# Moving the angle tables, pacing the linear work through two attentions, and adding the band term in VectorE's pass

## The chip, the cores and the metric

The kernel runs on one core of a Trainium2 chip. The metric is the device time of one execution in microseconds. Engines are named as in the profile: PE is TensorE (PEld its weight loads), DVE is VectorE, ACT is ScalarE, POOL is GpSimd, SP is SyncE, which only issues DMAs here.

## What is computed

The reference is two blocks over 512 positions of width 1024, all in fp32. The first block mixes a pooling branch and a causal block attention (8 heads) and has an MLP of width 4096 with a squared ReLU. The second has two layers: differential attention (8 heads of two softmaxes over all 512 keys), then windowed attention with 16 query heads, 4 key heads and a sink logit for each head; each layer is followed by a gated convolution MLP (2 x 2816) and a gated projection of a side input. The windowed attention, cut to what matters:

```
mask = (abs(kpos - qpos) <= 128) & (kpos >= 0) & (kpos < S)
s = where(mask, q k^T * d**-0.5, -inf)
m = maximum(max(s), sink)
e = exp(s - m)
pr = e / (sum(e) + exp(sink - m))
o = pr v
```

## The kernel before

Every large product is made of three fp32r matmuls: each operand is split into a high and a low half (`w_split`, `split`: the high half by ScalarE or GpSimd, the low by VectorE's subtraction), and `mm3` (lines 102 to 107) adds high x high, low x high and high x low in a PSUM bank. Activations lie transposed, 1024 features in eight tiles of 128 x 512 positions. `linear_steps` (line 123) walks over the output columns, 128 at a time: for each it loads and splits weights some tiles ahead (four high and four low buffers), makes 8 x 3 matmuls of 512 columns, and evacuates. It is a generator and yields after each `mm3`.

PSUM has tags: `mm` (2 banks), `sc` (2, scores), `pv` (1, values), `st` (1, statistics), `tr` (2, transposes). `wide` says which of them a linear product may use: 5 is all of `mm`, `sc`, `pv`; 1 is `mm` alone; 4 is `mm` and `sc`.

In both attentions of the second block, `weave` (line 163) writes linear work (`lin()`) between attention steps (`att()`). A list of points (step, us) says how much linear work, in an estimate of its own (648 ns for one `mm3`), has been written when a step is reached. Marks hold either side back: `("sq", g, i)` says that a head's queries are written, `"scored"` and `"scored2"` that the last scores are, `("o", k)` and `("so", k)` that a tile of the attention's output is. This sets the order of the program text. The framework that builds the program plans each engine's order from it: what is written first goes first, and an engine that would stand idle in the plan takes later work that is ready.

The angle tables for the rotations (`late_consts`, line 261) are made by VectorE and two sines on ScalarE and stored to DRAM. They are written behind the first of four up-projections of the first MLP (line 762). The rows of the convolution weights are loaded next (line 764) and transposed behind the second up-projection (line 766); the tables' buffers lie where these rows' buffers come to lie after them. Behind the first four columns of the first up-projection `mid` writes the statistics of the norm, and the fifth bank takes the fifth column meanwhile.

In the windowed attention one step of 64 handles 128 queries of one head against 256 or 384 keys. `scores` (line 1131) makes two matmuls of scores, and a third one that adds the band (0 inside, -1e30 outside) as identity x band, over those blocks that the band cuts. VectorE then negates the scores and takes the minimum together with the negated sink (line 1150), ScalarE makes the exponential from the bank and its sum (line 1152). After every second step the sink's exponential, the sum and the reciprocal are made for two steps together (lines 1156 to 1158), and GpSimd scales the two probability tiles. Those are a ring of six (`pr`). `flip` transposes them five steps after their scores, `values` multiplies with V once for a head. Queries and keys are rotated in `rope` (line 800), with DMAs that swap halves, and restacked by further DMAs. The residual stream is spilled to DRAM during each attention and reloaded by `unspill`.

Of the kernel before, what the change touches and what calls it, by code (L numbers as in the profile page):

```python
# [17 lines left out]
KT = D // 128  # L18
# [15 lines left out]
class Net:  # L34
# [647 lines left out]
    def block1(self):  # L682
# [58 lines left out]
        with tc.tile_pool(name="mlp", bufs=1) as M:  # L741
# [4 lines left out]
            for g in range(FF1 // 1024):  # L746
# [14 lines left out]
                if g == 0:  # L761
                    self.late_consts()
                    cv = ExitStack()
                    rows = self.conv_rows(cv.enter_context(tc.tile_pool(name="cv", bufs=1)))
                if g == 1:
                    self.conv_cols(rows)
                    cv.close()
                if g == 3:
                    self.sq_start()
# [108 lines left out]
    def diff(self):  # L878
# [4 lines left out]
        with tc.tile_pool(name="diff", bufs=1) as P:  # L883
# [17 lines left out]
            def lin():  # L901
                for h in range(KT):
                    if h != 1:
                        yield from qk(h)
                    if h in (0, 1, 4, 6):
                        i = (0, 1, 4, 6).index(h)
                        if i >= 2:
                            yield ("dvfree", i - 2)
                        yield from vv(i)
                yield "scored"  # L910
                self.unspill()
                self.wide = 4
                yield from self.linear_steps(a["diff_w_o_2"][0], o, [n * 128 for n in range(KT)], evac_o, group=3,
                                             ready=lambda k: ("o", k))
# [96 lines left out]
            def att():  # L1011
                for g in range(39):
                    yield g
                    if g < 32:
# [6 lines left out]
                        if g == 31:  # L1021
                            self.marks.add("scored")
# [24 lines left out]
            self.weave(att(), lin(), [(0, 50), (24, 125), (28, 126), (34, 134), (38, 139)])  # L1047
            self.wide = 5

    def swa(self):  # L1050
# [5 lines left out]
        with tc.tile_pool(name="swa", bufs=1) as P:  # L1056
            sink = P.tile([128, 4 * HQ], F32, name="sink")[:, :HQ]
            nc.scalar.dma_start(sink, a["swa_sinks_2"].to_broadcast([128, HQ]))
            identr = P.tile([128, 128], F32R, name="identr")
            nc.vector.tensor_copy(identr, self.ident)  # L1060
            nsink = P.tile([128, 4 * HQ], F32, name="nsink")[:, :HQ]
            nc.vector.tensor_scalar(nsink, sink, -1.0, None, op0=OP.mult)
            band = P.tile([128, 384], F32R, name="band")
            z = P.tile([128, 384], F32, name="pr", tag="pr", bufs=6)
            nc.gpsimd.memset(z, 0.0)
            nc.gpsimd.affine_select(z, z, pattern=[[1, 384]], compare_op=OP.is_ge, fill=NEG, base=0,
                                    channel_multiplier=-1)
            nc.gpsimd.affine_select(band, z, pattern=[[-1, 384]], compare_op=OP.is_ge, fill=NEG, base=256,
# [47 lines left out]
            def lin():  # L1116
                yield from self.linear_steps(w, self.u, [1024, 1152], evac_k, group=2)
                yield from q_steps(0, 0)
                yield from self.v_steps(w, 1280, rs()[0], lambda t: (V[:, t, :, 0], V[:, t, :, 1]), self.u)
                for g, j in ((0, 1), (1, 0), (1, 1)):  # L1120
                    yield from q_steps(g, j)
                yield "scored2"
                self.unspill()
                self.wide = 4
                yield from self.linear_steps(a["swa_w_o_2"][0], o, [n * 128 for n in range(KT)], evac_o, group=3,
# [5 lines left out]
            def scores(n, t):  # L1131
# [11 lines left out]
                for step in range(2):  # L1143
                    self.dots(sc, Q[g, i], K[g], s, qs, ks, step)
                blk = lambda x: x.rearrange("p (b q) -> p b q", q=128)
                m0, m1 = (1 if t == 0 else 0), (1 if t == NT - 1 else b1 - b0)
                c = b0 - t + 1
                nc.tensor.matmul(blk(sc)[:, m0:m1:2], identr, blk(band)[:, c + m0:c + m1:2], start=False, stop=True)
                p = P.tile([128, 384], F32, name="pr", tag="pr", bufs=6)
                nc.vector.tensor_scalar(p[:, :w_], sc, -1.0, nsink[:, h:h + 1], op0=OP.mult, op1=OP.min,  # L1150
                                        accum_out=st[:, 1, t:t + 1])
                nc.scalar.activation(p[:, :w_], sc, AF.Exp, bias=st[:, 1, t:t + 1], accum_out=st[:, 2, t:t + 1])  # L1152
                PR[n, t] = p
                if t % 2:
                    ts = slice(t - 1, t + 1)
# [3 lines left out]
                    for t_ in (t - 1, t):  # L1159
# [39 lines left out]
            def att():  # L1199
                done = []  # L1200
                for g in range(70):
                    yield g
                    if g < 64:
# [6 lines left out]
                        if g == 63:  # L1210
                            self.marks.add("scored2")
# [4 lines left out]
                    if g >= 9 and (g - 9) % 4 == 0:  # L1216
                        n = (g - 9) // 4
                        values(n)
# [16 lines left out]
            self.weave(att(), lin(), [(0, 35), (50, 63), (63, 63), (69, 85)])  # L1235
# [285 lines left out]
```

## Time and profile before

| what | value |
| --- | --- |
| time, median of 3 runs | 2008.62 us (2007.45 to 2009.44) |
| profiled execution | 2005.98 us |
| its span, first to last instruction | 2004.2 us |
| TensorE busy | 1955.9 us |
| VectorE busy | 1262.3 us |
| ScalarE busy | 799.9 us |
| GpSimd busy | 443.8 us |
| mean granted TensorE clock | 0.997 |

Busy time is the union of an engine's instructions. Matmuls are pipelined and their ends are modelled, so the distance from one start to the next says more than a duration. In a row, what stands behind `<-` at the end is what the engine had waited for.

### The profile page before, as it was taken

Reading aid. Unit: us, or ns where it says so; the run is one execution under the profiler, and the core shown is the slowest. Engines: PE = TensorE matmul, PEld = TensorE weight load, DVE = VectorE, ACT = ScalarE, POOL = GpSimd, SP = SyncE. Lnnn points to the kernel's source line nnn. Section 1 sums busy time; section 2 is a strip of 40 time slices with the busy share of each in tenths; the row PEclk is TensorE's granted clock in tenths of the full one; section 3 lists DMA queues with packets and bytes.
Section 4 is the critical chain, followed back from the end, with each engine's and each line's share of the span. In section 5 each row is a group of like instructions: output and inputs, shape, how many; then the busy total and the mean of one; then the engine's idle time right before and its main releaser. Section 6 shows DMA issues by size and latency. Waiting matters only on the chain.

```text
span 2004.2 us, 25430 instructions
## 1 busy us (share of the span) xinstructions
PE 1955.9 (98%) x9386; PEld 1621.8 (81%) x9386; DVE 1262.3 (63%) x2087; ACT 799.9 (40%) x1392; POOL 443.8 (22%) x545
## 2 busy tenths in 40 slices
PE   8999999899999999999999999999998999999997
PEld 6897778787888887887788888887877788888886
DVE  6447655534434468988684565668798684565665
ACT  4335434322212445554342331334575342342342
POOL 4125421000000211110221113122343221113122
PEclk9999999999999999999999999999999999999999
DMA  5263543332323356543332323335522333334231
GB/s 195 85 171 77 157 135 120 107 105 80 110 86 104 116 173 154 129 128 93 102 106 87 106 87 102 90 121 168 141 78 89 85 105 105 94 96 143 78 105 63
DMA packets 263853, 224.33 MB, mean 112 GB/s; under 512 B 9957, under 2 KB 236338, under 8 KB 263730
## 3 DMA queue, kind: packets, MB, share of 16 engines
q1 hardware_dynamic: 260538, 218.19, 36.7%
q10 hardware_dynamic: 3192, 4.52, 0.7%
q8 instruction: 74, 1.21, 0.3%
q14 instruction: 49, 0.40, 0.1%
HBM read 182.83 MB, written 14.16 MB: 98 GB/s over the span
## 4 chain that ended last, share of the span: by engine, by line
PE 51%; DVE 6%; ACT 2%; issue 1%; DMA 1%; SPq 0%; POOL 0%; DVEq 0%; ACTq 0%; POOLq 0%
PE mm L105 7%; PE mm L107 7%; PE mm L106 7%; PE sc L107 6%; PE sc L105 6%; PE sc L106 6%; PE pv L105 3%; PE pv L106 3%; PE pv L107 3%; PE sc L849 1%; DVE wlo L94 1%; PE pv L858 1%; ACT pr L1152 1%; DVE Tl L80 1%; DVE st L955 0%
## 5 line engine op out<-in xcount | busy, mean ns | idle before, releaser
L94 DVE TENSOR_TENSOR wlo<-wst,whi 128x1024 fp32r<-128x1024 f32 (+2 forms) x304 | 392.1, 1293 | 196.2 <-ACT whi L93 145.4
L93 ACT ACTIVATE whi<-wst 128x1024 fp32r<-128x1024 f32 (+2 forms) x203 | 207.2, 1026 | 459.9 <-PE sc L106 176.1
L105 PE MATMUL mm<-uh,whi 128*128 128x512 f32 x712 | 281.7, 396 | 2.2 <-DVE t L751 2.2
L106 PE MATMUL mm<-ul,whi 128*128 128x512 f32 x712 | 279.1, 392 | 1.1 <-DVE ul L83 1.1
L91 POOL TENSOR_SCALAR whi<-wst 128x1024 fp32r<-128x1024 f32 (+2 forms) x101 | 110.2, 1091 | 766.0 <-PE sc L106 234.6
L107 PE MATMUL mm<-uh,wlo 128*128 128x512 f32 x712 | 279.1, 392 | 0.0
L106 PE MATMUL sc<-ul,whi 128*128 128x512 f32 x488 | 190.7, 391 | 0.6 <-DVE ul L83 0.6
L105 PE MATMUL sc<-uh,whi 128*128 128x512 f32 x488 | 191.1, 392 | 0.0
L107 PE MATMUL sc<-uh,wlo 128*128 128x512 f32 x488 | 190.5, 390 | 0.0
L105 PEld LDWEIGHTS mm<-uh,whi 128*128 128x128 f32 x712 | 134.4, 189 | 28.1 <-DVE t L751 2.4
L107 PEld LDWEIGHTS mm<-uh,wlo 128*128 128x128 f32 x712 | 134.1, 188 | 27.3
L106 PEld LDWEIGHTS mm<-ul,whi 128*128 128x128 f32 x712 | 134.4, 189 | 26.7 <-DVE ul L83 1.6
L107 PEld LDWEIGHTS sc<-uh,wlo 128*128 128x128 f32 x488 | 91.8, 188 | 19.9 <-DVE wlo L94 0.7
L106 PEld LDWEIGHTS sc<-ul,whi 128*128 128x128 f32 x488 | 91.9, 188 | 19.5 <-DVE ul L83 0.9
L105 PEld LDWEIGHTS sc<-uh,whi 128*128 128x128 f32 x488 | 91.9, 188 | 18.9 <-ACT uh L82 0.2
L105 PE MATMUL sc<-ah,whi 128*128 128x512 f32 x264 | 102.9, 390 | 0.0
L106 PE MATMUL sc<-al,whi 128*128 128x512 f32 x264 | 102.8, 389 | 0.0
L107 PE MATMUL sc<-ah,wlo 128*128 128x512 f32 x264 | 102.7, 389 | 0.0
L107 PE MATMUL pv<-uh,wlo 128*128 128x512 f32 x256 | 99.9, 390 | 2.1 <-DVE wlo L94 2.1
L105 PE MATMUL pv<-uh,whi 128*128 128x512 f32 x256 | 100.4, 392 | 0.0
L106 PE MATMUL pv<-ul,whi 128*128 128x512 f32 x256 | 99.7, 389 | 0.0
L1260 ACT ACTIVATE cv<-cu,cc 128x512 f32<-128x512 f32 x88 | 70.9, 813 | 60.5 <-DVE cu L1258 59.6
(458 smaller groups left out, 4299.8 us busy)
## 6 DMA issues: line engine op xcount, KB each, us to landing
wst<-ffn_w_up SPq DMA_DIRECT2D x88, 512.0 KB
wst<-w_up SPq DMA_DIRECT2D x16, 1024.0 KB
wst<-w_down SPq DMA_DIRECT2D x16, 1024.0 KB
wst<-ffn_w_down SPq DMA_DIRECT2D x16, 1024.0 KB
wst<-w_in SPq DMA_DIRECT2D x16, 512.0 KB
wst<-w_in SPq DMA_DIRECT2D x8, 1024.0 KB
wst<-diff_w_qkv SPq DMA_DIRECT2D x16, 512.0 KB
wst<-ple_w_gate SPq DMA_DIRECT2D x8, 1024.0 KB
```

The source lines that it names most:

```text
L80: nc.vector.tensor_tensor(lo, src, f32(hi), op=OP.subtract)
L91: nc.gpsimd.tensor_scalar(hi, src, 1.0, 1.0, op0=OP.mult, op1=OP.mult)
L93: nc.scalar.activation(hi, src, AF.Copy)
L94: nc.vector.tensor_tensor(lo, src, f32(hi), op=OP.subtract)
L105: nc.tensor.matmul(ps, ah, bh, start=first, stop=False)
L106: nc.tensor.matmul(ps, ah, bl, start=False, stop=False)
L107: nc.tensor.matmul(ps, al, bh, start=False, stop=last)
L849: self.nc.tensor.matmul(ps, q[m][:, qs], k[2 * step + m][:, ks], start=step == 0, stop=last and step == 1)
L858: nc.tensor.matmul(*args, start=first and x == 0, stop=last and x == 1)
L1152: nc.scalar.activation(p[:, :w_], sc, AF.Exp, bias=st[:, 1, t:t + 1], accum_out=st[:, 2, t:t + 1])
L1260: nc.scalar.activation(v, u[:, 1:S + 1], AF.Identity, bias=cc[:, 3, ft:ft + 1], scale=cc[:, 1, ft:ft + 1])
```

## The change

Four edits.

1. `late_consts()` is written behind the second up-projection and the convolution rows' transposes, not behind the first up-projection.
2. Differential attention: the value projections are made with heads 0, 2, 4, 6 (they were with 0, 1, 4, 6). The output projection no longer waits for the mark `"scored"`; its first group has two columns instead of three. `unspill` and `wide = 4` are written in the attention, at the last score. The points of the pace are new.
3. Windowed attention: the same for its output projection, and new points. The first `values` waits in the text for a new mark, `"sv"`, that V is written.
4. Windowed attention: no band matmul. The band is an fp32 tile in SBUF, and VectorE's pass is `tensor_tensor_reduce`: it adds the band to the scores, negates, writes the result, and takes the minimum with the negated sink. The exponential reads that result. The sink's exponential, sum and reciprocal are made once for the four steps of a head, and then GpSimd scales four tiles.

```diff
                 if g == 0:
-                    self.late_consts()
                     cv = ExitStack()
                     rows = self.conv_rows(cv.enter_context(tc.tile_pool(name="cv", bufs=1)))
                 if g == 1:
                     self.conv_cols(rows)
                     cv.close()
+                    self.late_consts()
...
-                    if h in (0, 1, 4, 6):
-                        i = (0, 1, 4, 6).index(h)
+                    if h in (0, 2, 4, 6):
+                        i = h // 2
...
-                yield "scored"
-                self.unspill()
-                self.wide = 4
-                yield from self.linear_steps(a["diff_w_o_2"][0], o, [n * 128 for n in range(KT)], evac_o, group=3,
-                                             ready=lambda k: ("o", k))
+                yield from self.linear_steps(a["diff_w_o_2"][0], o, [n * 128 for n in range(KT)], evac_o, first=2,
+                                             group=3, ready=lambda k: ("o", k))
...
                         if g == 31:
-                            self.marks.add("scored")
+                            self.unspill()
+                            self.wide = 4
...
-            self.weave(att(), lin(), [(0, 50), (24, 125), (28, 126), (34, 134), (38, 139)])
+            self.weave(att(), lin(), [(0, 32), (10, 62), (18, 93), (26, 125.3), (34, 133), (38, 139)])
...
                 for step in range(2):
-                    self.dots(sc, Q[g, i], K[g], s, qs, ks, step)
-                blk = lambda x: x.rearrange("p (b q) -> p b q", q=128)
-                m0, m1 = (1 if t == 0 else 0), (1 if t == NT - 1 else b1 - b0)
-                c = b0 - t + 1
-                nc.tensor.matmul(blk(sc)[:, m0:m1:2], identr, blk(band)[:, c + m0:c + m1:2], start=False, stop=True)
+                    self.dots(sc, Q[g, i], K[g], s, qs, ks, step, True)
+                c = (b0 - t + 1) * 128
                 p = P.tile([128, 384], F32, name="pr", tag="pr", bufs=6)
-                nc.vector.tensor_scalar(p[:, :w_], sc, -1.0, nsink[:, h:h + 1], op0=OP.mult, op1=OP.min,
-                                        accum_out=st[:, 1, t:t + 1])
-                nc.scalar.activation(p[:, :w_], sc, AF.Exp, bias=st[:, 1, t:t + 1], accum_out=st[:, 2, t:t + 1])
+                nc.vector.tensor_tensor_reduce(p[:, :w_], sc, band[:, c:c + w_], -1.0, nsink[:, h:h + 1], OP.add, OP.min,
+                                               st[:, 1, t:t + 1])
+                nc.scalar.activation(p[:, :w_], p[:, :w_], AF.Exp, bias=st[:, 1, t:t + 1], scale=-1.0,
+                                     accum_out=st[:, 2, t:t + 1])
                 PR[n, t] = p
-                if t % 2:
-                    ts = slice(t - 1, t + 1)
+                if t == NT - 1:
+                    ts = slice(0, NT)
...
-            self.weave(att(), lin(), [(0, 35), (50, 63), (63, 63), (69, 85)])
+            self.weave(att(), lin(), [(0, 22), (9, 32), (15, 42), (30, 52), (46, 63), (63, 70), (69, 85)])
```

## Rows read from the trace of the kernel before

**Rows 1.** The page's first part: busy time of each engine, its share of the span, and its instructions.

```profile
PE 1955.9 (98%) x9386; PEld 1621.8 (81%) x9386; DVE 1262.3 (63%) x2087; ACT 799.9 (40%) x1392; POOL 443.8 (22%) x545
```

**Rows 2.** Busy time by stretch, in columns: stretch, its length, then for PE, PEld, DVE, ACT and POOL the busy us and instructions, the granted clock, the DMA share, GB/s. The stretches are the one around the first MLP's start, three plain groups of its projections, the differential attention, the windowed attention, and a part of the latter.

```profile
350.00:375.00 25.00, 19.48 (x84) 15.42 (x83) 21.03 (x40) 10.70 (x15) 2.25 (x2) 0.93 0.40 137
400.00:720.00 320.00, 319.66 (x1416) 263.04 (x1416) 142.57 (x181) 97.41 (x138) 30.70 (x25) 1.00 0.33 108
760.00:940.00 180.00, 175.26 (x1021) 148.55 (x1021) 160.31 (x352) 101.05 (x221) 26.39 (x19) 1.00 0.51 135
1432.00:1545.00 113.00, 102.95 (x601) 84.86 (x601) 102.10 (x305) 81.42 (x251) 48.56 (x85) 0.98 0.35 99
1500.00:1525.00 25.00, 19.91 (x114) 15.74 (x112) 22.10 (x69) 18.72 (x58) 9.98 (x19) 0.93 0.23 64
```

**Rows 3.** TensorE's waits over the whole span: instruction, what released it, us in total, times, longest.

```profile
PE sc L849 <- ACT pr L1152: 3.9, 7, 2.0
```

**Rows 4.** TensorE's instructions in order of time around 360 us: start, us, engine, line, operation, tiles, shape, count, and in brackets the idle time before and its releaser. The fifth column's first matmul, its third, the transposes that broadcast the norm, and the first and eighth matmul of the next column.

```profile
358.05 0.49 PE L105 MATMUL pv<-uh,whi 128*128 128x512 f32 x1
...
360.92 0.50 PE L107 MATMUL pv<-uh,wlo 128*128 128x512 f32 x1 [2.15 <-DVE wlo L94]
...
367.43 0.62 PE L330 MATMUL st<-ident,ny 128*128 128x128 f32 x4 [1.22 <-DVE ny L316]
370.21 0.79 PE L105 MATMUL mm<-uh,whi 128*128 128x512 f32 x1 [2.16 <-DVE t L751]
...
373.29 0.40 PE L106 MATMUL mm<-ul,whi 128*128 128x512 f32 x1
```

**Rows 5.** The same view of VectorE and ScalarE: the first table instruction, the subtraction of the weight's low half, the first step of the norm's statistics, the copy of the broadcast norm, the first evacuation.

```profile
352.88 0.43 DVE L270 CAST ang<-pos 128x512 f32<-128x512 int32 x1 [2.95 <-issue]
...
359.65 2.35 DVE L94 TENSOR_TENSOR wlo<-wst,whi 128x1024 fp32r<-128x1024 f32 x2
361.92 0.15 DVE L354 TENSOR_SCALAR nx<-st 128x4 f32<-128x4 f32 x1
...
368.20 0.58 ACT L362 ACTIVATE R<-st 128x512 f32<-128x512 f32 x1
...
369.47 0.68 DVE L751 SCALAR_TENSOR_TENSOR t<-mm,R 128x512 f32<-128x512 f32 x1
```

**Rows 6.** VectorE's groups between 346 and 372 us: the costliest and the cheapest of the nine groups of table work (lines 270 to 286), which sum to 9.4 us: 2.3, 1.6, 1.4, four of 0.8, 0.5 and 0.4. Columns: line, engine, operation, tiles, shapes, count, busy us, mean ns, idle us before and its releaser.

```profile
L283 DVE SCALAR_TENSOR_TENSOR red<-kk,ang 128x512 f32<-128x512 f32 x2 | 2.3, 1134 | 0.0
...
L270 DVE CAST ang<-pos 128x512 f32<-128x512 int32 x1 | 0.4, 426 | 2.9 <-issue 2.9
```

**Rows 7.** VectorE in order of time behind the small transposes: its next instruction, with the idle time before it.

```profile
492.78 0.69 DVE L775 TENSOR_TENSOR y<-pv,y 128x512 f32<-128x512 f32 x1 [11.37 <-PE pv L107]
```

**Rows 8.** TensorE in order of time at the first scores of the windowed attention: two band matmuls, each with the matmul that started next.

```profile
1433.63 0.22 PE L1148 MATMUL sc<-band,identr 128*128 128x128 f32 x1
1433.69 0.39 PE L849 MATMUL sc<-st,st 128*128 128x384 f32 x1
...
1434.09 0.28 PE L1148 MATMUL sc<-band,identr 128*128 128x256 f32 x1
1434.20 0.34 PE L849 MATMUL sc<-st,st 128*128 128x384 f32 x1
```

**Rows 9.** VectorE's groups by shape: the pass over the scores in the windowed attention (line 1150), and the two-tensor pass in the first block's attention (line 625).

```profile
L1150 DVE TENSOR_SCALAR_CACHE_REDUCE pr<-sc,nsink 128x384 f32<-128x384 f32 x32 | 19.4, 608 | 4.2 <-PE sc L1148 2.3 <-POOL pr L1162 1.7 <-PE sc L849 0.2
L1150 DVE TENSOR_SCALAR_CACHE_REDUCE pr<-sc,nsink 128x256 f32<-128x256 f32 x32 | 15.3, 477 | 0.3
...
L625 DVE CUSTOM_DVE_ANT_0 pr<-sc,bias 128x384 f32<-128x384 f32 x8 | 4.4, 550 | 2.0 <-POOL pr L629 1.6 <-POOL bias L603 0.4
L625 DVE CUSTOM_DVE_ANT_0 pr<-sc,bias 128x256 f32<-128x256 f32 x8 | 3.3, 418 | 0.2
```

**Rows 10.** The same view: the exponential from the score bank and, in the first block, from SBUF; the sink's exponential, the sum and the reciprocal.

```profile
L1152 ACT ACTIVATE pr<-sc,st 128x384 f32<-128x384 f32 x32 | 18.5, 578 | 2.3 <-DVE pr L1150 2.1
...
L626 ACT ACTIVATE pr<-pr,st 128x384 f32<-128x384 f32 x8 | 4.9, 612 | 3.5 <-DVE st L625 3.5
...
L1156 ACT ACTIVATE st<-st,sink 128x2 f32<-128x2 f32 x32 | 9.3, 291 | 0.0
...
L1157 DVE TENSOR_TENSOR st<-st 128x2 f32<-128x2 f32 x32 | 5.6, 176 | 1.0 <-ACT st L1156 0.7
...
L1158 DVE RECIPROCAL st<-st 128x2 f32<-128x2 f32 x32 | 5.0, 156 | 0.1
```

**Rows 11.** VectorE in order of time: the first low half of the windowed attention's output projection.

```profile
1524.41 1.21 DVE L94 TENSOR_TENSOR wlo<-wst,whi 128x1024 fp32r<-128x1024 f32 x1
```

**Rows 12.** TensorE in order of time: the first score of the windowed attention.

```profile
1433.20 0.36 PE L849 MATMUL sc<-st,st 128*128 128x256 f32 x1 [1.19 <-DMA st<-ql]
```

**Rows 13.** VectorE, GpSimd and TensorE in order of time: the first pass of all, the fourth pass of one head, the scaling of its third and fourth tile, the transposes of the third, and the last pass of all.

```profile
1433.89 0.48 DVE L1150 TENSOR_SCALAR_CACHE_REDUCE pr<-sc,nsink 128x256 f32<-128x256 f32 x1
...
1505.78 0.48 DVE L1150 TENSOR_SCALAR_CACHE_REDUCE pr<-sc,nsink 128x256 f32<-128x256 f32 x1
...
1507.82 1.04 POOL L1162 TENSOR_SCALAR pr<-pr,st 128x384 f32<-128x384 f32 x2 [2.04 <-ACT Th L79]
...
1508.60 0.49 PE L1175 MATMUL tr<-ident,pr 128*128 128x128 f32 x3
...
1540.86 0.48 DVE L1150 TENSOR_SCALAR_CACHE_REDUCE pr<-sc,nsink 128x256 f32<-128x256 f32 x1
```

More of the change, by code (lines that the diff above doesn't have):

```diff
@@ L1058, in swa @@
             nc.scalar.dma_start(sink, a["swa_sinks_2"].to_broadcast([128, HQ]))
-            identr = P.tile([128, 128], F32R, name="identr")
-            nc.vector.tensor_copy(identr, self.ident)
             nsink = P.tile([128, 4 * HQ], F32, name="nsink")[:, :HQ]
             nc.vector.tensor_scalar(nsink, sink, -1.0, None, op0=OP.mult)
[L1063 to L1066, printed above, removed]
+            band = P.tile([128, 384], F32, name="band")
+            nc.gpsimd.memset(band, 0.0)
+            nc.gpsimd.affine_select(band, band, pattern=[[1, 384]], compare_op=OP.is_ge, fill=NEG, base=0,
                                     channel_multiplier=-1)
-            nc.gpsimd.affine_select(band, z, pattern=[[-1, 384]], compare_op=OP.is_ge, fill=NEG, base=256,
+            nc.gpsimd.affine_select(band, band, pattern=[[-1, 384]], compare_op=OP.is_ge, fill=NEG, base=256,
                                     channel_multiplier=1)
@@ L1119, in lin @@
                 yield from self.v_steps(w, 1280, rs()[0], lambda t: (V[:, t, :, 0], V[:, t, :, 1]), self.u)
+                self.marks.add("sv")
                 for g, j in ((0, 1), (1, 0), (1, 1)):
                     yield from q_steps(g, j)
[L1122 to L1125, printed above, removed]
+                yield from self.linear_steps(a["swa_w_o_2"][0], o, [n * 128 for n in range(KT)], evac_o, first=2, group=3,
                                              order=[0, 1, 2, 3, 4, 6, 5, 7], ready=lambda k: ("so", k))
@@ L1158, in scores @@
                     nc.vector.reciprocal(st[:, 4, ts], st[:, 4, ts])
-                    for t_ in (t - 1, t):
+                    for t_ in range(NT):
                         b0, b1 = span(t_)
@@ L1210, in att @@
                         if g == 63:
-                            self.marks.add("scored2")
+                            self.unspill()
+                            self.wide = 4
                         yield (640.0, 880.0, 880.0, 640.0)[t] * 0.75
@@ L1217, in att @@
                         n = (g - 9) // 4
+                        yield "sv"
                         values(n)
```

## The prediction

> **What bounds the kernel now.** I read the page's busy shares first: TensorE is busy for 98% of the span [rows 1]. So the time is TensorE's work plus the places where it waits, and a change can only shorten it by taking matmuls away or by filling waits. The stretches come next [rows 2]: in the plain up- and down-projections (400 to 720 us) TensorE is busy for 319.66 of 320 us, so nothing can be gained there. It lacks 4.7 us in the differential attention (760 to 940), 10.05 us in the windowed attention (1432 to 1545), and 5.5 us in the 25 us around 360 us. Two of the stretches have a granted clock of 0.93. In the windowed attention VectorE is busy for 102.1 of 113 us, and in 1500 to 1525 for 22.1 of 25 while TensorE has only 19.9: there VectorE sets the pace. TensorE's own waits are last [rows 3]: the longest in the windowed attention is for the exponential that still reads a score bank.
>
> The sum is made against the profiled execution, 2005.98 us (span 2004.2 and 1.8 around it). It is 0.13% below the median of the runs, 2008.62, so a difference that I find there is taken off the median unchanged.
>
> **The change, part by part.**
>
> *The angle tables move* from behind the first up-projection group to behind the second. Around 360 us TensorE starts a column of 24 matmuls at 358.05, and its next column only at 370.21 [rows 4]. The column itself needs 24 x 0.2275 = 5.5 us and the four transposes 0.4, so 6.3 us are lost. Two waits make them: for the low half of a weight (its subtraction starts at 359.65, because VectorE was working on the tables from 352.9) and then for the chain of the norm's statistics, which starts at 361.92 with table work between its steps [rows 5]. Behind it the clock is at the lower of its two levels: the seven matmul starts from 370.21 to 373.29 take 3.1 us where 1.6 would do, 1.5 us more. Together 7.8 us. Without the tables the subtraction can follow its high half at once, and the statistics can be ready when the column ends at 363.5. What is late next is the broadcast of the norm: from the transposes (367.43) over the copy (368.20) to the release of the bank (370.15) took 2.7 us, of which 0.6 was another subtraction in front. About 2.2 us stay. Gain 7.8 - 2.2 = 5.6; the ends are 7.8 and 0 (below nothing if the new place hurts). At the new place the tables need 9.4 us of VectorE [rows 6], two ScalarE passes, and the issue of their loads and stores on ScalarE's queue. They lie behind the eight small transposes that free their buffers, which end at 481.4; from there VectorE sat idle for 11.37 us [rows 7]. That gap hides them. The eight loads of the convolution's rows now come ahead of them on ScalarE's queue, and ScalarE was busy for 10.7 of the 25 us there [rows 2]. If the loads push the work 4 us past its end, it competes with weight splitting that runs a column ahead, so I cost it at nothing; if the cover were gone it would be up to 3 us.
>
> *The band term* leaves TensorE: 64 matmuls, half with 128 columns and half with 256. From start to next start they take 0.06 and 0.11 to 0.12 us [rows 8], so 32 x 0.06 + 32 x 0.115 = 5.6 us. TensorE's work is on the path nearly everywhere, so I take all of it; the lower end is 0, if VectorE sets the pace throughout.
>
> *The maximum pass* now adds the band. The same kind of pass stands in the first block's attention. It takes 550 and 418 ns for 384 and 256 columns, the pass that goes away 608 and 477 [rows 9]: 58 ns less, 64 x 0.058 = 3.7 us of VectorE, and the read of the accumulator stays. The exponential then reads that pass's result and not the score bank: 612 against 578 ns at 384 columns [rows 10], 64 x 0.036 = 2.3 us more of ScalarE, which was busy for 81 of 113 us [rows 2]. But the score bank is free one exponential earlier, so TensorE's 3.9 us of waits for it [rows 3] go; what is late next is the pass itself in VectorE's queue.
>
> [...]
>
> *The sink sums* come once for a head: 16 fewer exponentials of 291 ns, sums of 176 and reciprocals of 156 [rows 10], 5.3 us of VectorE and 4.7 of ScalarE. GpSimd scales the same 64 tiles, but in bursts of four, and the first tile of a head waits for the fourth.
>
> *The paced weaving.* VectorE's load in 1432 to 1545 falls from 102.1 by 3.7 + 5.3 to about 93 us, while TensorE's is 103 - 5.6. The waste there is 10.05 us of idle TensorE and, in 1500 to 1525, 7% of the clock, 1.75 us: 11.8. In that stretch nothing linear was left: the output projection's first low half was subtracted only at 1524.41 [rows 11], since that projection was written behind the last score. Now its first two columns are written from step 46 on, in banks that the scores don't use. I take half, 6 us, since the beginning can't move: the first score waited for a transfer of the rotated queries at 1433.20 [rows 12], which an earlier place in the text doesn't hasten. Ends 11.8 and 0, and below nothing by the last rival. In the differential attention the same holds for its start; its output projection's first group shrinks from three to two and takes no score bank. Of its 4.7 us I take 2; ends 4.7 and, if the shifted linear work collides, a loss of as much.
>
> *The rest:* the eight reloads of the residual stream on SyncE's queue are written at the last score instead of behind a mark. They need the buffers of the last heads' queries and keys, which no edit frees sooner, and the first reader is the output projection's end. One small cast goes. I cost these at nothing, with up to 1 us if a weight's load has to stand behind the eight.
>
> Sum: 5.6 + 5.6 + 6 + 2 = 19.2 us, so 2008.6 - 19.2 = 1989.4.
>
> **Rivals.**
>
> *The weaving changes nothing:* the order on each engine is planned and already moves later work into gaps, and the attention starts when its data is there. For it: the first score waited for a transfer, not for TensorE. Against it: 1500 to 1525, where no linear work was ready. Then 5.6 + 5.6: 1997.4.
>
> *All waits in both attentions go:* 5.6 + 5.6 + 11.8 + 4.7 = 27.7, so 1980.9. For it: VectorE falls below TensorE in load. Against: the tail of each attention is a chain with nothing beside it.
>
> *The tables don't leave:* they are lifted early again, or their burst delays the second down-projection by as much as it saves. For it: they were lifted once, ahead of where they are written. Against: their buffers follow those of the small transposes. Then 19.2 - 5.6: 1995.0.
>
> *The ring of six probability tiles binds (the slower side).* A head's four tiles stay unscaled until its fourth is done, so the next head can only fill two before it waits for the first tile's transposes. Now a head takes 6.8 us: (1540.86 - 1433.89) / 63 x 4 [rows 13]. With the ring as the bound it takes the chain from the fourth pass to the first tile's transposes, and one pass more. One such chain of now: pass at 1505.78, scaling from 1507.82, transposes 1508.60 to 1509.1 [rows 13], 3.3 us; then the ring does not bind. But VectorE is 90% busy and each of five handoffs may wait for an instruction ahead: at 7.2 us of chain a head takes 7.8 us, 16 us lost, and with the tables' 5.6 and the 2 gained it ends at 2008.6 + 16 - 7.6 = 2017. It decides where 16 heads cost more than 7.6: above 7.3 us a head, a chain of 6.7 us, twice the one shown.
>
> **How the numbers follow.** Forecast 0.52, weaving nothing 0.20, all waits gone 0.13, tables stay 0.07, ring 0.08. Two thousandths, 4 us, is about what a measurement of this kernel tells from no change, so no change is 2004.6 to 2012.6. Slower is the ring, 0.08. No change gets a quarter of the second case (a ring that binds for a few heads takes back 7 us), 0.05, a third of the tables' case, 0.02, and 0.03 of the forecast's upper tail, together 0.10; faster is 0.82. The range from 1978 to 2005 leaves out the ring, a little of the no-change cases, and what lies below full filling, some 2 in 10.
>
> **What would show it.** Tables: TensorE without a gap over 3 us between 355 and 372 us, a clock of 1.0 there, and the table work of VectorE in the gap before the second down-projection; wrong if the gap stays or a new one stands near 490. Band: TensorE has 64 fewer matmuls; the new pass near 550 and 418 ns, wrong at 608 and over. Score bank: the wait of scores on the windowed exponential is gone. Weaving: matmuls of the output projection within the stretch from the 40th to the 64th score step, the clock 1.0 there, TensorE's idle time in the windowed attention under 5 us. Ring: VectorE's new pass waits for transposes or for GpSimd's scaling by more than 1.7 us in total. The prediction fails if the idle time of TensorE in the windowed attention is not at least halved, or if a new idle stretch opens elsewhere.

## The result and the profile after

The changed kernel took 2024.88 us (median of 4 runs, 2021.12 to 2025.45) beside 2009.03 for the kernel before: ratio 1.0076, 95% interval 1.0061 to 1.0091, slower by 0.76%. The forecast was 1989.4, the range 1978 to 2005. The profiled execution took 2024.69 us.

TensorE has 64 fewer matmuls, as the band's edit asks, and yet its busy time is 2.7 us longer: its mean granted clock was 0.993 (0.997 in the kernel before), and at the lower clock matmuls take longer (behind the gap at 743 us, below, they start 0.43 us apart instead of 0.23). The first part of the page after, against [rows 1]:

```profile
PE 1958.6 (97%) x9322; PEld 1618.7 (80%) x9322; DVE 1261.6 (62%) x2054; ACT 800.6 (40%) x1376; POOL 447.5 (22%) x545
```

By stretch, with the columns of [rows 2]: the place that the tables left, the place that they went to, the start and the end of the differential attention, the windowed attention.

```profile
340.00:375.00 35.00, 33.94 (x156) 27.69 (x155) 26.44 (x49) 16.53 (x25) 2.25 (x2) 1.00 0.26 83
475.00:500.00 25.00, 25.00 (x112) 20.71 (x111) 17.16 (x26) 5.72 (x6) 3.57 (x2) 1.00 0.43 139
720.00:760.00 40.00, 33.37 (x191) 28.91 (x190) 23.20 (x36) 14.62 (x23) 10.28 (x6) 0.91 0.54 139
920.00:960.00 40.00, 32.85 (x172) 25.14 (x172) 25.11 (x74) 14.77 (x33) 1.00 (x1) 0.94 0.33 98
1447.00:1561.00 114.00, 99.08 (x530) 77.42 (x530) 98.78 (x269) 80.92 (x233) 49.34 (x81) 0.97 0.35 96
```

The gap around 360 us is gone and none has opened around 490. The loss stands in the next two rows: TensorE is idle for 6.6 and 7.2 of 40 us, at a granted clock of 0.91 and 0.94. In the kernel before it was idle for 1.0 and 1.3 us in these stretches, at 1.00:

```profile
720.00:760.00 40.00, 38.96 (x267) 36.11 (x267) 25.79 (x48) 17.38 (x27) 8.04 (x5) 1.00 0.49 129
920.00:960.00 40.00, 38.75 (x207) 30.31 (x205) 29.82 (x83) 20.57 (x42) 2.39 (x2) 1.00 0.21 60
```

The windowed attention has 14.9 us of idle TensorE where it had 10.05.

TensorE's waits, as in [rows 3] (instruction, releaser, total, times, longest):

```profile
PE mm L105 <- ACT rx L804: 6.4, 2, 5.7
PE tr L1166 <- POOL pr L1153: 6.1, 8, 1.6
...
PE sc L849 <- DVE st L1140: 3.4, 6, 1.3
```

The wait for the windowed exponential is gone, and 3.4 us of wait for the new pass (now line 1140) stand in its place. The new pass by shape, and the exponential behind it (columns as in [rows 9]):

```profile
L1140 DVE CUSTOM_DVE_ANT_0 pr<-sc,band,nsink 128x384 f32<-128x384 f32 x32 | 19.5, 612 | 5.1 <-POOL pr L1153 4.7
L1140 DVE CUSTOM_DVE_ANT_0 pr<-sc,band,nsink 128x256 f32<-128x256 f32 x32 | 15.1, 474 | 0.8 <-PE tr L1166 0.4 <-POOL Th L1160 0.2
...
L1142 ACT ACTIVATE pr<-pr,st 128x384 f32<-128x384 f32 x32 | 19.6, 612 | 1.2 <-DVE st L1140 1.0
```

612 and 474 ns, not 550 and 418; and the pass waits for GpSimd's scaling for 4.7 us, where the old one waited 1.7.

TensorE in order of time at the two idle places of the differential attention (columns as in [rows 4]): four instructions at its start, then four near its end.

```profile
742.84 0.39 PE L107 MATMUL mm<-uh,wlo 128*128 128x512 f32 x1
748.93 0.80 PE L105 MATMUL mm<-uh,whi 128*128 128x512 f32 x1 [5.70 <-ACT rx L804]
749.52 0.63 PE L106 MATMUL mm<-ul,whi 128*128 128x512 f32 x1
749.95 0.63 PE L107 MATMUL mm<-uh,wlo 128*128 128x512 f32 x1
...
917.71 0.39 PE L849 MATMUL sc<-dm,st 128*128 128x512 f32 x1
...
931.34 0.40 PE L107 MATMUL mm<-oh,wlo 128*128 128x512 f32 x1
933.48 0.29 PE L330 MATMUL st<-ident,sy 128*128 128x128 f32 x1 [1.74 <-DVE sy L316]
933.60 0.71 PE L849 MATMUL sc<-st,st 128*128 128x512 f32 x2
```

At the start a linear column waits 5.7 us for a bank that ScalarE still has to drain, and behind it matmuls start 0.43 us apart instead of 0.23: the lower clock, granted at 0.50 from 749 to 754. At the end the last score of head 6 starts at 917.71 and the first of head 7 at 933.60, a gap of 15.9 us. In the kernel before the gap was 3.6 us:

```profile
920.02 0.39 PE L849 MATMUL sc<-dm,st 128*128 128x512 f32 x1
...
923.60 0.62 PE L849 MATMUL sc<-st,st 128*128 128x512 f32 x2
```

What head 7 waited for, in order of time on four engines, after its last linear matmul had ended at 911.5: drain, swap of halves, rotation, low half, last restacking.

```profile
913.59 0.58 ACT L804 ACTIVATE rx<-mm 128x512 f32<-128x512 f32 x1
...
916.88 1.22 SPq L808 DMA_DIRECT2D rs<-rx  x2
...
919.72 1.29 POOL L809 TENSOR_TENSOR rs<-rs,R 128x512 f32<-128x512 f32 x1 [7.24 <-DMA rs<-rx]
...
923.14 0.68 DVE L80 TENSOR_TENSOR dl<-rx,st 128x512 fp32r<-128x512 f32 x1
...
929.87 0.47 SPq L842 DMA_DIRECT2D dl<-dl  x1
```

So head 7's keys need 22 us here from their last matmul to the first score. In the kernel before it was 19.4 us (from 904.2 to 923.60), but there that matmul ended 15.8 us ahead of head 6's last score, here 6.2.

### The profile page after: what moved, and what is told of

It reads as the page before. It is cut to its first block, busy times and chain, and to the rows that moved or that the text cites. A ratio compares the mean times of both kernels' runs of the same rounds, so it can differ in the third digit from the quotient of the medians.

```text
span 2022.9 us, 25215 instructions
## 1 busy us (share of the span) xinstructions
PE 1958.6 (97%) x9322; PEld 1618.7 (80%) x9322; DVE 1261.6 (62%) x2054; ACT 800.6 (40%) x1376; POOL 447.5 (22%) x545
## 4 chain that ended last, share of the span: by engine, by line
PE 82%; DVE 9%; issue 3%; ACT 2%; DMA 2%; POOL 2%; SPq 0%; DVEq 0%; POOLq 0%; ACTq 0%
PE mm L105 12%; PE mm L107 11%; PE mm L106 11%; PE sc L105 9%; PE sc L107 9%; PE sc L106 9%; PE pv L106 5%; PE pv L105 5%; PE pv L107 5%; PE sc L849 2%; DVE wlo L94 1%; POOL pr L1153 1%; DVE Tl L80 1%; PE st L322 1%; PE pv L858 1%
## 5 line engine op out<-in xcount | busy, mean ns | idle before, releaser
L105 PE MATMUL mm<-uh,whi 128*128 128x512 f32 x720 | 286.6, 398 | 6.3 <-ACT rx L804 5.7
L105 PE MATMUL sc<-uh,whi 128*128 128x512 f32 x512 | 200.8, 392 | 0.0
L107 PE MATMUL sc<-uh,wlo 128*128 128x512 f32 x512 | 199.9, 390 | 0.8 <-DVE wlo L94 0.8
L106 PE MATMUL sc<-ul,whi 128*128 128x512 f32 x512 | 200.0, 391 | 0.6 <-DVE ul L83 0.6
L106 PEld LDWEIGHTS sc<-ul,whi 128*128 128x128 f32 x512 | 96.3, 188 | 20.5 <-DVE ul L83 1.1
L1266 POOL TENSOR_TENSOR cv<-cv 128x512 f32<-128x512 f32 x44 | 57.6, 1309 | 167.8 <-DVE cv L1256 167.3
L345 POOL TENSOR_TENSOR acc<-acc,sq 128x512 f32<-128x512 f32 x48 | 72.2, 1504 | 99.0 <-ACT sq L343 99.0
L107 PE MATMUL mm<-ah,wlo 128*128 128x512 f32 x236 | 91.9, 389 | 0.0
L105 PE MATMUL sc<-ah,whi 128*128 128x512 f32 x236 | 91.9, 389 | 0.0
L107 PE MATMUL sc<-ah,wlo 128*128 128x512 f32 x236 | 91.8, 389 | 0.0
L106 PE MATMUL mm<-al,whi 128*128 128x512 f32 x236 | 91.8, 389 | 0.0
```

The source lines that it names most:

```text
L105: nc.tensor.matmul(ps, ah, bh, start=first, stop=False)
L106: nc.tensor.matmul(ps, ah, bl, start=False, stop=False)
L107: nc.tensor.matmul(ps, al, bh, start=False, stop=last)
L345: eng.tensor_tensor(self.acc, self.acc, sq, op=OP.add)
L1266: nc.gpsimd.tensor_tensor(v, v, gt[f], op=OP.mult)
```

## Experiments

"Beside before" is the difference of the medians of a run and of the kernel before in the same batch; a negative one is faster. It was +15.9 us for the changed kernel. In brackets stand a run's ratio to the kernel before and its 95% interval. An interval reaches 2 to 4 us to either side, so a step between two runs carries 3 to 5 us of noise, and steps of 1 to 3 us are not clear of it. Each expectation gives the time by a theory and by a rival to it.

**The change in four steps.** `e1_tables` has edit 1 alone:

```diff
                 if g == 0:
-                    self.late_consts()
...
                     cv.close()
+                    self.late_consts()
```

> The kernel before with the angle tables moved and nothing else. In the changed kernel the first rotation of the differential attention starts 7.6 us earlier on GpSimd than before (732.70 against 740.34), though the rest of the kernel is slower. Theory (the loss lies in the weaving): this edit alone is worth 6 to 8 us, about 2002. Rival (the gain ahead of 740 us belongs to the earlier text of the attention): 0 to 2 us, about 2008.

2000.0 us, ratio 0.9961 (0.9946 to 0.9975), -7.9 beside before. The theory held.

`e2_band` has the band in VectorE's pass and nothing else of the change (the exponential reads the pass's result):

```diff
-                nc.tensor.matmul(blk(sc)[:, m0:m1:2], identr, blk(band)[:, c + m0:c + m1:2], start=False, stop=True)
...
-                nc.vector.tensor_scalar(p[:, :w_], sc, -1.0, nsink[:, h:h + 1], op0=OP.mult, op1=OP.min,
+                nc.vector.tensor_tensor_reduce(p[:, :w_], sc, band[:, c:c + w_], -1.0, nsink[:, h:h + 1], OP.add, OP.min,
```

> The kernel before with the band added in VectorE's pass, sink sums still after every second step, weaving as before. Theory (TensorE's work is on the path, the pass is no longer than the old one): 4 to 6 us faster than before, about 2004. Rival (the windowed attention goes at VectorE's pace, whose pass takes 612 and 474 ns in the changed kernel and so saves nothing): within 2 us of before.

2014.97 us, ratio 1.0037 (1.0024 to 1.0050), +7.1 beside before: neither the theory nor the rival had it.

`e3_no_weave` has tables, band and sink sums with the old weaving (`if t % 2` becomes `if t == NT - 1`), and `e4_swa_weave` that and the new weaving of the windowed attention:

> The changed kernel with the weaving of before in both attentions: tables, band and sink sums stay. Theory (all of the loss is in the weaving): 1994 to 1999, that is 6 to 8 us for the tables and 4 to 6 for the band below before. Rival (the ring of six probability tiles, held for a whole head, costs the windowed attention its gain): 2001 to 2008, and VectorE's pass waits over 4 us for GpSimd's scaling or for transposes.

> The changed kernel with the weaving of before in the differential attention alone. From the changed kernel's trace that attention lost 21 us: its first output tile is added at 962.0 against 954.4 after a start that was 7.6 ahead, the last at 992.8 against 979.3. Theory (linear work is confined to two banks from 32 us on, and the first output group has two columns): about 2004, 20 below the changed kernel. Rival (its loss is shared with the windowed attention's): 2010 to 2018.

`e3_no_weave` took 2004.32 us (0.9973, 0.9962 to 0.9984), -3.6: the rival's time, and its passes wait 5.8 us for scaling and transposes. `e4_swa_weave` took 2005.30 us (0.9991, 0.9982 to 1.0001), -2.6, near its theory. In steps: tables -7.9, band +7.1, sink sums -2.8 (what is left of -3.6 beside the first two), windowed weaving +1.0, differential weaving 15.9 + 2.6 = +18.5. The tables, the band and the differential weaving are clear of the noise, the other two are not.

**Why the band costs.** Its two halves, each alone, on the kernel before. `e5_no_band` leaves the band matmuls out and adds the band nowhere:

> The kernel before without the 64 band matmuls, and the band added nowhere: the mask is left out, VectorE's pass and the exponential stay as they were. Theory (VectorE sets the pace of the windowed attention, 0.9 to 0.98 busy there, and the band matmuls ran in time that TensorE had left; without them the plan brings linear columns forward, TensorE runs dry later beside the same VectorE work and falls to half clock): 2 to 8 us slower than the kernel before, so 2010 to 2016, with two or more windows at half clock between 1440 and 1545 us. Rival (the new pass and its shared buffer cost the 7 us of e2_band; the matmuls were on the path, as predicted): 4 to 6 us faster, 2002 to 2004.

2015.09 us (1.0030, 1.0019 to 1.0041), +6.9: the theory. `e6_band_twice` keeps the matmuls and has the new pass too:

> The kernel before with its band matmuls kept and the new VectorE pass besides (the band is added twice, the exponential reads SBUF). Theory: the pass costs what the old one did, so within 2 us of the kernel before, 2006 to 2010. Rival (the pass, its buffer held through the exponential, or the exponential from SBUF cost): 5 to 13 us slower, 2013 to 2021.

2016.70 us (1.0039, 1.0025 to 1.0053), +8.5: the rival by its number. So each half costs about what both cost together, and the cost is not a sum of the two. `e12_const_init` changes one operand of `e2_band`:

```diff
-... band[:, c:c + w_], -1.0, nsink[:, h:h + 1], OP.add, OP.min,
+... band[:, c:c + w_], -1.0, 3e38, OP.add, OP.min,
```

> e2_band with a constant where the minimum starts, instead of the pointer to the head's negated sink; the sink is left out of the maximum. Theory (the pointer costs the pass its 58 ns, and VectorE sets the length of the windowed attention): the pass takes 550 and 418 ns, the 64 passes span 3 to 5 us less than e2_band's 104.0 us, and the time is 2009 to 2013 beside e2_band's 2015. Rival 1 (the pass costs 612 and 474 ns with a constant too): no change, 2013 to 2017. Rival 2 (the pass gets shorter, but something else sets the length): 550 and 418 ns, and 2013 to 2017.

2008.03 us (0.9996, 0.9985 to 1.0008), +0.4 beside before and 6.7 less than `e2_band`; this is just below the theory's 2009 to 2013. The pass by shape, in `e2_band` and then in this kernel (columns as in [rows 9]):

```profile
L1144 DVE CUSTOM_DVE_ANT_0 pr<-sc,band,nsink 128x384 f32<-128x384 f32 x32 | 19.4, 607 | 0.2 <-PE tr L1170 0.2
L1144 DVE CUSTOM_DVE_ANT_0 pr<-sc,band,nsink 128x256 f32<-128x256 f32 x32 | 15.2, 477 | 0.9 <-PE tr L1170 0.6 <-POOL pr L1157 0.2
```

```profile
L1144 DVE CUSTOM_DVE_ANT_0 pr<-sc,band 128x384 f32<-128x384 f32 x32 | 17.5, 548 | 1.6 <-POOL pr L1157 1.0 <-PE tr L1170 0.4
L1144 DVE CUSTOM_DVE_ANT_0 pr<-sc,band 128x256 f32<-128x256 f32 x32 | 13.3, 417 | 3.3 <-PE sc L849 1.8 <-PE tr L1170 1.2
```

The pointer to a start value (the address of one value per partition, in place of a constant) costs about 60 ns a pass. From the first pass to the last the 64 take 107.0 us in the kernel before, 104.0, 106.8 and 105.4 in `e2_band`, `e5_no_band` and `e6_band_twice`, and 99.7 here: leaving the matmuls out hardly changes that length, a shorter pass of VectorE does. The band matmuls ran in time that TensorE had left over. Busy time between 1430 and 1545 us, in the kernel before, in `e2_band` and in `e12_const_init` (columns as in [rows 2]):

```profile
1430.00:1545.00 115.00, 104.95 (x609) 86.18 (x609) 102.10 (x305) 82.93 (x253) 48.56 (x85) 0.99 0.35 99
```

```profile
1430.00:1545.00 115.00, 98.72 (x522) 76.99 (x521) 102.54 (x305) 85.42 (x253) 48.60 (x84) 0.95 0.31 83
```

```profile
1430.00:1545.00 115.00, 102.60 (x555) 80.51 (x554) 101.07 (x310) 85.57 (x254) 51.79 (x86) 0.97 0.36 97
```

What went from TensorE came back as idle time (16.3 us in `e2_band`, 10.05 before) and as lower clock: 0.04 x 115 = 4.6 us of full-speed time in `e2_band`. This is not the luck of one profile. Over all executions the mean granted clock is 0.9952 in the kernel before (21 runs, 0.993 to 0.997), 0.9922 in `e2_band` (6 runs, 0.990 to 0.994) and 0.9926 in `e5_no_band`; 0.0030 of 2013 us is 6 us, by this estimate most of the 7.1.

Why TensorE falls idle is seen when the stretch is cut in two, in the kernel before and then in `e5_no_band`:

```profile
1430.00:1475.00 45.00, 41.97 (x252) 35.07 (x252) 39.55 (x121) 35.84 (x106) 19.22 (x32) 1.00 0.40 101
1475.00:1545.00 70.00, 62.98 (x357) 51.11 (x358) 62.55 (x186) 47.09 (x148) 29.34 (x53) 0.98 0.32 98
```

```profile
1430.00:1475.00 45.00, 43.41 (x235) 34.98 (x234) 39.20 (x110) 33.69 (x94) 19.56 (x31) 1.00 0.43 110
1475.00:1545.00 70.00, 56.89 (x289) 43.06 (x288) 62.69 (x189) 48.53 (x153) 26.24 (x51) 0.90 0.25 70
```

The linear work moved forward. By a count in the traces (lines 105 to 107) 67 of its matmuls start in the first part and 85 in the second in the kernel before; 103 and 33 in `e5_no_band`, 99 and 32 in `e2_band`, 80 and 48 in `e6_band_twice` (104 and 59 in `e12_const_init`, where the attention is shorter). So the late heads have little beside them: the output projection had 27 matmuls done by 1540 us in the kernel before, and 6, 4 and 4 in `e2_band`, `e5_no_band` and `e6_band_twice`. That the planned order does this, as the expectation of `e5_no_band` said, fits; no run holds the order fixed. Why `e6_band_twice` costs 8.5 us stays open in part: its pass takes what the old one took (609 and 476 ns), and its clock, 0.9936, accounts by the same estimate for some 3 us.

**The two places of the differential attention.** `e7_start_50` tried the start point of the pace, and `e8_first_3` the group's size, each on the changed kernel:

```diff
-            self.weave(att(), lin(), [(0, 32), (10, 62), (18, 93), ...
+            self.weave(att(), lin(), [(0, 50), (10, 62), (18, 93), ...
```

> The changed kernel, with 50 us of linear work ahead of the differential attention instead of 32, the rest of its pace as it is. Theory (with 32 us the columns behind the first head's find only the two mm banks, still held until ScalarE has drained them, and TensorE stands 5.7 us and then runs 6.8 us at half clock): 7 to 11 us faster than the changed kernel, 2014 to 2018, with the wait of mm on ScalarE's drain gone. Rival (the loss sits in the rest of the attention, and a later start costs what the banks give): within 3 us of the changed kernel, 2022 to 2027.

2019.83 us (1.0059, 1.0044 to 1.0074), +11.6: between the theory and the rival, hardly clear of the noise, and with the same wait of 5.7 us. In the new order head 2's columns come right behind the first value columns, and they hold the linear work until head 0's scores are written, so 50 us of it can't be written ahead.

> The changed kernel with a first group of three columns in the differential attention's output projection instead of two. Theory (two columns offer 16 mm3 beside the last heads where three offered 24, 8 x 0.65 = 5 us of filler less, and TensorE falls to half clock twice there): 5 to 10 us faster than the changed kernel, 2015 to 2020, with no half clock between 920 and 965 us. Rival (the linear work that was spread earlier is what lacks at the end, a third column does not make up for it): within 3 us, 2022 to 2027.

2025.27 us (1.0081, 1.0062 to 1.0100), +17.1: the theory missed. The next three came from reading these traces: the last head's keys, the old order of the value columns, both.

```diff
-            ... (18, 93), (26, 125.3), (34, 133), (38, 139)])
+            ... (18, 93), (24, 125.3), (34, 133), (38, 139)])
```

> The changed kernel, with the last head's queries and keys of the differential attention written by step 24 (as in the kernel before) instead of step 26; nothing else. Theory (the last head's key column ended at 911.5 us, its drain, rotation and stacking took until 933 us, and the scores of head 7 stood until then, with too little linear work beside): 5 to 10 us faster than the changed kernel, 2015 to 2020, with no gap between the scores of heads 6 and 7 and the stalls of 920 to 960 us (12.5 us) down to 4 to 6. Rival (the two columns of the first group of the output projection are what lacks there): within 3 us, 2022 to 2027.

2015.27 us (1.0043, 1.0028 to 1.0058), +7.6, the theory; and the gap ahead of head 7 is 3.8 us.

```diff
-                    if h in (0, 2, 4, 6):
-                        i = h // 2
+                    if h in (0, 1, 4, 6):
+                        i = (0, 1, 4, 6).index(h)
...
-            self.weave(att(), lin(), [(0, 32), (10, 62), (18, 93), ...
+            self.weave(att(), lin(), [(0, 50), (10, 62), (18, 93), ...
```

> The changed kernel with the old order of the value columns (heads 0, 1, 4, 6) and 50 us of linear work ahead of the differential attention. Theory (with the new order head 2's columns come behind the first value columns, and these wait for a bank until ScalarE has drained the first keys, and then for a mark; the second value columns filled that time): stalls between 740 and 780 us (12 us in the changed kernel) down to 3 to 5, so 7 to 10 us faster, 2015 to 2018. Rival (the loss is set by the tables and rotations that the attention waits for, whatever stands beside): within 3 us of e7_start_50, 2017 to 2022, with the stall kept.

2015.57 us (1.0042, 1.0027 to 1.0057), +7.9, the theory. This run changes the order and the start together; the old order with the start at 32 us was not run.

> Both edits of e9_last_keys and e10_vv_start at once. Theory (the whole loss of the differential attention, 19.6 us by e4_swa_weave, is these two places): 2004 to 2010, near e4_swa_weave. Rival (even linear work in the middle of the attention costs too): 2011 to 2017.

2008.06 us (1.0003, 0.9993 to 1.0012), +0.4. The theory held, and the two mends add up: 8.3 and 8.0 us alone, 15.5 together, of the 18.5. Busy time by stretch in this kernel:

```profile
740.00:780.00 40.00, 36.74 (x216) 31.03 (x216) 31.39 (x49) 19.14 (x39) 10.57 (x7) 1.00 0.56 146
900.00:960.00 60.00, 56.56 (x310) 45.16 (x309) 49.01 (x117) 32.03 (x66) 5.92 (x5) 1.00 0.33 95
```

The clock is 1.00 in both.

**The sink sums and the ring.** With the sums once a head the 64 passes span 112.5 us in `e3_no_weave`, 8.5 more than in `e2_band`, though VectorE has less to do. `e13_ring_8` is `e3_no_weave` with a ring of four for the outer tiles of a head (256 columns) and one of four for the inner; the sink and its negation share a tile to make room:

```diff
-                p = P.tile([128, 384], F32, name="pr", tag="pr", bufs=6)
+                wide = (256, 384)[0 < t < NT - 1]
+                p = P.tile([128, wide], F32, name="pr", tag="pr%d" % wide, bufs=4)
```

> e3_no_weave with a ring of eight pr tiles (four of 384 columns, four of 256) instead of six, all else equal. Theory (sink sums once a head hold four tiles until the head's last exponential, so with six the next head's passes wait for transposes; VectorE sets the pace): the 64 passes span 100 to 106 us instead of 112.5, and the time falls from 2004.3 to 1997 to 2001. Rival (the span comes from the plan's order, not from the ring): 110 us and over, 2003 to 2006.

2003.62 us (0.9975, 0.9965 to 0.9985), -4.8; the passes span 107.9 us, between the theory and the rival. The larger ring took back about half of the 8.5, and the time hardly moved (-1.2): the rival's number. `e14_sinks` is `e1_tables` with the sums once a head:

> e1_tables with sink sums once a head, the band still on TensorE, a ring of six. Theory of the ring: the passes span 110 to 114 us as in e3_no_weave, and the time is that of e1_tables or above, 2000 to 2005. Rival (5.3 us less VectorE work counts in full, the ring is no bound): 1994 to 1997.

2003.18 us (0.9974, 0.9964 to 0.9984), -5.3, a span of 111.3. The theory held. With the old pass the sink sums cost 2.6 us by the medians, where they gained 2.8 beside the new pass; neither is clear of the noise.

**What is left of the change.** `e15_best` joins the edits of `e12_const_init` and `e13_ring_8`; `e16_repaired` is the changed kernel with these and the mends of `e11_both`. In both the sink is left out of the maximum that is subtracted (it stays in the sum).

> Tables moved, band in VectorE's pass with a constant where the minimum starts (the sink is left out of the maximum), sink sums once a head, a ring of eight, the old weaving. Theory (VectorE's passes set the windowed attention): e13_ring_8 less 3 to 7 us, 1991 to 1997, the passes spanning 95 to 102 us. Rival (TensorE and the plan's order set it by then): the time of e13_ring_8, within 2 us.

2001.07 us (0.9961, 0.9948 to 0.9974), -7.4; the span was 100.3 us, within the theory, but the time is only 2.6 us below `e13_ring_8`, between the theory (3 to 7) and the rival (within 2).

> The whole changed kernel with four mends: the old order of the value columns and 50 us ahead, the last head's keys by step 24, a constant where the minimum starts, a ring of eight. Theory (what is left of the new weaving is worth nothing, e11_both less e4_swa_weave being 2.8 us): e15_best plus 1 to 5 us, 1993 to 2001. Rival (the new weaving pays once the attention is short enough to need filling): 1 to 6 us below e15_best.

1997.06 us (0.9946, 0.9929 to 0.9964), -11.4, 4.0 below `e15_best`: the rival. Four of the five runs of `e15_best` lie above all of these. Its windowed attention:

```profile
1430.00:1545.00 115.00, 106.10 (x586) 82.46 (x585) 101.56 (x283) 84.54 (x243) 50.49 (x86) 1.00 0.35 95
```

The clock is 1.00 (0.96 in `e15_best`, 4.6 us of full-speed time), and linear matmuls start in every 15 us of the stretch; in `e15_best` none does between 1505 and 1520. Two more runs divide this gain: `e17_weave_only` has the mended weaving on the tables alone, `e18_sink_kept` puts the pointer back.

> e1_tables with both new weavings, that of the differential attention mended (old order of the value columns, 50 us ahead, the last head's keys by step 24); band on TensorE, sink sums by pairs. Theory (the mended weaving is worth the 4 us between e15_best and e16_repaired by itself): 1995 to 1998. Rival (it pays only where VectorE's passes are short; in e11_both it cost 2.8 us): 2000 to 2005.

2001.36 us (0.9965, 0.9951 to 0.9980), -6.7: no gain over `e1_tables`, the rival.

> e16_repaired with the pointer to the negated sink where the minimum starts, so with the sink in the maximum. Theory (the pointer's 60 ns by 64 lengthen VectorE's passes, and these set the length): the passes span 104 to 110 us instead of 99.5, and the time is 2000 to 2004. Rival (the ring of eight and the weaving have moved the limit to TensorE): 1996 to 1999.

2005.28 us (0.9982, 0.9972 to 0.9991), -2.8, a span of 106.0 us, as the theory had it: the pointer costs this kernel 8.6 us, and the time is above the theory's 2000 to 2004.

## Why the prediction was wrong

The forecast was -19.2 us and +15.9 came, 35.1 apart. The differential attention accounts for 20.5 of that (-2 forecast, +18.5 measured), the band for 12.7 (-5.6, +7.1), the weaving and the sink sums of the windowed attention for 4.2 (-6, -1.8), and the tables take back 2.3.

*Tables:* right, and the term was too small, 5.6 against 7.9. "About 2.2 us stay" was too much: TensorE is idle for 1.06 us between 340 and 375, since transposes of other rows now stand between the statistics and the next column.

*Band matmuls:* the step "TensorE's work is on the path nearly everywhere, so I take all of it" failed. The other end, 0, was named with its condition (VectorE sets the pace throughout), [rows 2] showed VectorE busy for 102.1 of 113 us, and `e5_no_band` went beyond it: +6.9.

*Pass:* "58 ns less" failed: the pass took 612 and 474 ns where the old one took 608 and 477. The two passes of [rows 9] differ in an operand: the row of line 625 reads scores and bias alone, its minimum starts from a constant, and the new pass reads the sinks too. With a constant in that place (`e12_const_init`) the new pass took 548 and 417 ns, within 2 ns of that row.

*Score bank:* the wait on the exponential went and its place was taken by "the pass itself in VectorE's queue", as the text said (3.9 us before, 3.4 after). By its own rows the exponential's 0.036 should read 0.034; that enters no sum.

*Sink sums:* VectorE's and ScalarE's savings came (16 sums of 176 and 16 reciprocals of 171 ns instead of 32 each), but a head now holds its tiles until its fourth exponential. That is the ring of the last rival, given 0.08. The mark set for it (over 1.7 us of waits for scaling) was passed, at 4.7; its price of 16 us was too high: a larger ring gave back 1.2 us in `e13_ring_8`, within the noise.

*Windowed weaving:* -6 forecast, +1.0 in place. The projection's matmuls stood beside the last heads as asked, but they had stood there with the old weaving too (44 of them by 1540 us in `e4_swa_weave`, 36 in `e3_no_weave`). Idle time and clock did not improve (100.4 us busy between 1430 and 1545 at 0.97, 100.8 at 0.96), and the passes span 111.5 us against 112.5: the attention had not become shorter. With a shorter pass and a larger ring both new weavings together, mended, gave 4.0 us (`e16_repaired`).

*Differential attention:* "Of its 4.7 us I take 2" failed by 20 us, and its lower bound, "a loss of as much", was no bound. The edit moves two things past queues that I did not follow: head 2's columns to a place where the keys of the first two heads still hold a bank (a wait of 5.7 us; 8 us in all, with the start of the pace), and the last head's keys behind two more steps, though from their last matmul to the first score lies a chain of 22 us over ScalarE, GpSimd, VectorE and two rounds of DMAs (8 us lost). What the edit added, 18.5 us, was not bounded by the 4.7 us of waits that were there. The 3.0 us between `e11_both` and `e4_swa_weave` stay open; they are not clear of the noise.

*Rivals:* the slower side held one mechanism, the ring, at 0.08, and the result on that side is not its doing. Three that were not named cost more: the freed time of TensorE beside VectorE, the value columns' order, the last keys.

## What to carry to other kernels

Where another engine sets a stretch's pace (VectorE here, busy for 90% of it), matmuls taken out of the stretch need not be worth anything, and may cost the clock (+6.9 us here, at 0.94 in that stretch where it was 0.99); shorten that engine's own instructions first. When linear work is spread more evenly, follow each column to its consumer: a key column is due by the length of its chain ahead of its scores (22 us here), and a column that is moved forward needs a bank that is already drained (a wait of 5.7 us here). Compare a price row's operands, not only its shape, before it is carried over.

## What the runs showed of the hardware

A VectorE pass over two tensors, one of them in PSUM, with a start value read per partition took 607 and 477 ns at 384 and 256 columns (`e2_band`), with a constant 548 and 417 (`e12_const_init`): some 60 ns for the operand, the same at both widths. In the windowed attention, where VectorE is busy for about 90%, those 64 x 0.06 = 3.8 us cost 6.7 us (`e2_band` to `e12_const_init`) and 8.6 (`e18_sink_kept` to `e16_repaired`), each with some 4 us of noise. The read of the accumulator behind each pass took another 82 ns, in the kernel before as in the changed one.

TensorE's granted clock was at its lower level where TensorE had stood idle: in the changed kernel, behind the wait of 5.7 us at 743 us, it was 0.50 from 749 to 754, with matmuls of 512 columns 0.43 us apart instead of 0.23. Between 1430 and 1545 us, beside a VectorE busy for 102.5 of the 115 us, it was 0.95 in `e2_band`, where TensorE was idle for 16.3 us, and beside one busy for 101.6 us it was 1.00 in `e16_repaired`, where TensorE was idle for 8.9. In `e5_no_band`, the kernel before without its 64 band matmuls, it was 0.94 with 14.7 us idle (0.99 with 10.05 in the kernel before), and the time was 6.9 us longer.
